# Moving a small-row store, recutting the last row and exchanging two waits at the end of a streaming row sum

## Chip, cores and metric

One core of one Trainium2 chip. Times are device microseconds (us) of that core, given as the median over runs. A run's time is about 1.35 us more than its *span*, from the first to the last instruction of the program; the profile shows the span. Trace times below count from the span's start; where three decimals stand, they are from the trace's records of instructions, packets and semaphore updates. In the views ACT is ScalarE, DVE is VectorE, and SPq and DVEq are the sequencers of SyncE and VectorE, which run waits and issue loads and stores; "issue" is time in which an engine waited for nothing that the profile shows. A *partial* is the sum of one piece of the last row; it is *announced* when its semaphore is updated, just after the short instruction that reads the accumulator out. A load or store has *landed* or is *complete* with the last of its 16 semaphore updates.

## The reference

```python
x = np.random.randn(32, 512, 1024).astype(np.float32)
def reference(x):
    return np.sum(np.maximum(x, 0), axis=-1).astype(np.float32)
```

16384 rows of 1024 numbers, 67.1 MB in and 64 KB out.

## The kernel before

Each of the 128 partitions takes 128 rows. They arrive in seven chunks of 16 rows, then in loads of 8, 4, 2 and 1 rows, and the very last row in three pieces of 512, 256 and 256 columns. All loads and stores are issued by SyncE on one queue. ScalarE sums the first piece of the last row; VectorE sums the second, then the third together with the two partial sums, which lie behind it in the same tile. Results leave in three stores: the middle rows (128 rows of 111 numbers, 444 bytes each), the first row of each partition (transposed, 4 rows of 128 bytes) and the last 16 rows (128 rows of 64 bytes).

```python
LAST = [512, 256, 256]
# ... loads of 8, 4, 2, 1 rows, then:
    parts = [buf[:, tb, r, 0:n0], buf[:, tb, r, n0:n1], last[:, 0 : LAST[2]]]
    for k, (lo, hi) in enumerate([(0, n0), (n0, n1), (n1, D)]):
        sp.dma_start(out=parts[k], in_=xv[-1][:, BIG - 1, lo:hi]).then_inc(
            s_in[NBIG + len(TAIL) + k], 16)
    sp.wait_ge(s_fact, 1)          # ScalarE is done with the big chunks
    sp.wait_ge(s_fdve, 1)          # VectorE too
    sp.dma_start(out=ov[1][:, :], in_=res[:, start[1] : start[2]]).then_inc(s_store, 16)
    sp.wait_ge(s_turn, 1)
    sp.dma_start(out=of[0:P].rearrange("(k q) -> k q", q=32),
                 in_=turned[0:P:32, 0:32]).then_inc(s_store, 16)
# ... all the work but the last row is cut ...
    n = LAST[2]
    act.wait_ge(s_in[-3], 16)
    on_act(parts[0], last[:, n : n + 1]).then_inc(s_part, 1)
    dve.wait_ge(s_in[-2], 16)
    on_dve(parts[1], last[:, n + 1 : n + 2]).then_inc(s_part, 1)
    dve.wait_ge(s_part, 2)
    dve.wait_ge(s_in[-1], 16)
    on_dve(last[:, :], res[:, J - 1 : J]).then_inc(s_tdve, 1)

    sp.wait_ge(s_tdve, 1)
    sp.dma_start(out=ov[-1][:, :], in_=res[:, start[-1] : J]).then_inc(s_out, 16)
    sp.wait_ge(s_store, 16 * (len(REGIONS) - 1))
    sp.wait_ge(s_out, 16)
```

In these programs' traces each computing or issuing instruction carries one wait at most. Of two waits in front of it, the one written *first* is built into the instruction, and the second becomes a wait instruction of its own ahead of it. So before the change VectorE waits separately for the last load, and its last instruction carries the wait for the two partials.

## Time and profile before

| | before |
|---|---|
| time, median of the first 3 runs (lowest to highest) | 161.03 us (160.97 to 161.25) |
| span of the profiled run | 159.908 us |

The prediction shows and reads the views of this profile: the chain of waits at the end, the timeline and the events of the last 2 us.

### The profile page before, as it was taken

The numbers are of one execution on the slowest core, as the hardware profiler recorded it, in microseconds if no ns is written. First come the engines' busy times: TensorE is split into PE (matmuls) and PEld (weight loads), VectorE is DVE, ScalarE is ACT, GpSimd is POOL, SyncE is SP. The second block draws the span as 40 slices with busy tenths as digits, with TensorE's granted clock in tenths as the row PEclk, the third lists the DMA queues.
The fourth block names the chain that finished last, engine by engine and source line by source line (L and its number), as shares of the span: only waits on it lengthen the run. The fifth ranks groups of instructions, "written<-read, shape, count | busy, mean of one in ns | idle before, by whom it ended". The sixth has DMA issues, their size and how long they took to land.

```text
span 159.9 us, 150 instructions
## 1 busy us (share of the span) xinstructions
DVE 121.5 (76%) x58; ACT 101.4 (63%) x55; POOL 0.2 (0%) x4
## 2 busy tenths in 40 slices
DVE  0000000999959999999969989699899999598995
ACT  3000059990799709996099942999339980496974
POOL 0000000000000000000000000000000000000000
DMA  9979996996996996997989969969969969899994
GB/s 377 492 338 400 492 525 262 525 525 262 525 525 262 525 525 262 525 459 328 525 361 426 525 262 525 525 262 525 525 262 525 525 262 525 369 418 393 408 381 148
DMA packets 2457, 67.18 MB, mean 420 GB/s; under 512 B 536, under 2 KB 792, under 8 KB 1176
## 3 DMA queue, kind: packets, MB, share of 16 engines
q1 hardware_dynamic: 2456, 67.18, 98.0%
q14 instruction: 1, 0.01, 0.0%
HBM read 67.11 MB, written 0.07 MB: 420 GB/s over the span
## 4 chain that ended last, share of the span: by engine, by line
DMA 68%; ACT 18%; DVE 11%; SPq 1%; issue 0%
DMA buf<-in_x_dram 68%; ACT buf L137 18%; DVE res L152 11%; SPq L98 1%; SPq L106 0%; DVE buf L122 0%; DVE last L122 0%
## 5 line engine op out<-in xcount | busy, mean ns | idle before, releaser
L152 DVE TENSOR_REDUCE res<-buf 128x7 f32<-128x7168 f32 (+4 forms) x16 | 100.0, 6281 | 33.7 <-ACT buf L137 33.7
L137 ACT ACTIVATE buf<-buf 128x7168 f32<-128x7168 f32 (+4 forms) x16 | 80.7, 5099 | 45.9 <-DMA buf<-in_x_dram 45.9
L119 ACT ACTIVATE buf<-buf 128x1024 f32<-128x1024 f32 (+1 forms) x19 | 19.0, 1000 | 9.3 <-DMA buf<-in_x_dram 9.3
L122 DVE TENSOR_SCALAR_CACHE_REDUCE buf<-buf 128x1024 f32<-128x1024 f32 (+2 forms) x19 | 20.9, 1147 | 3.1 <-DMA buf<-in_x_dram 2.9
L119 ACT ACTIVATION_READ_ACCUMULATOR buf<-buf 128x1 f32 x19 | 3.5, 186 | 0.0
L137 ACT ACT_TABLE_LOAD x1 | 1.3, 1283 | 1.3 <-PEq L216 1.3
L122 DVE DVE_READ_ACCUMULATOR buf<-buf 128x1 f32 x19 | 1.6, 84 | 0.0
L122 DVE TENSOR_SCALAR_CACHE_REDUCE last<-last 128x258 f32<-128x258 f32 x1 | 0.4, 422 | 0.0
L161 DVE STREAM_TRANSPOSE turned<-res 128x32 f32<-128x32 f32 x1 | 0.2, 211 | 0.0
L185 DVE TENSOR_TENSOR res<-half 128x1 f32<-128x1 f32 x1 | 0.2, 160 | 0.1
L216 POOL MEMSET const-bfloat16-1.0<- 128x1 bf16 x1 | 0.1, 102 | 0.0
L216 POOL MEMSET const-uint8-127<- 128x1 uint8 x1 | 0.1, 101 | 0.0
L216 POOL MEMSET const-float32-0.0<- 128x1 f32 x1 | 0.1, 99 | 0.2 <-issue 0.2
L216 POOL MEMSET const-float32-1.0<- 128x1 f32 x1 | 0.1, 98 | 0.0
L122 DVE DVE_READ_ACCUMULATOR last<-last 128x1 f32 x1 | 0.1, 83 | 0.0
## 6 DMA issues: line engine op xcount, KB each, us to landing
buf<-in_x_dram SPq DMA_DIRECT2D x1, 7680.0 KB, 21.2
buf<-in_x_dram SPq DMA_DIRECT2D x1, 4096.0 KB, 26.8
buf<-in_x_dram SPq DMA_DIRECT2D x1, 2048.0 KB, 31.3
buf<-in_x_dram SPq DMA_DIRECT2D x2, 512.0 KB, 18.9
buf<-in_x_dram SPq DMA_DIRECT2D x1, 1024.0 KB, 33.3
buf<-in_x_dram SPq DMA_DIRECT2D x1, 256.0 KB, 34.5
buf<-in_x_dram SPq DMA_DIRECT2D x1, 128.0 KB, 34.4
last<-in_x_dram SPq DMA_DIRECT2D x1, 128.0 KB, 34.2
```

The source lines that it names most:

```text
L98: sp.dma_start(out=buf[:, tb, r : r + n, :], in_=xv[-1][:, r : r + n, :]).then_inc(s_in[NBIG + i], 16)
L119: return act.activation(t, t, AF.Relu, accum_out=acc)
L122: return dve.tensor_scalar(out=t, in0=t, scalar1=0.0, scalar2=None, op0=ALU.max, op1=ALU.add, accum_out=acc)
L137: act.activation(t, t, AF.Relu).then_inc(s_act, 1)
L152: dve.tensor_reduce(out=res[:, c * BIG + r : c * BIG + r + n], in_=buf[:, c % NB, r : r + n, :], axis=X, op=ALU.add,).then_inc(s_dve, 1)
L161: dve.transpose(out=turned[:, :], in_=res[:, 0:32]).then_inc(s_turn, 1)
L185: dve.tensor_tensor(out=res[:, j0 + r : j0 + r + 1], in0=half[:, 0:1], in1=half[:, 1:2], op=ALU.add)
L216: nc = _bacc.Bacc("TRN2", target_bir_lowering=False, num_devices=1)
```

## The change

Its intent, as the diff shows it: keep the packets of 444 bytes out of the end of the load stream, have the second piece of the last row sooner, and let VectorE's last instruction answer the last load at once. Line numbers and blank lines apart, this is the whole diff:

```diff
-LAST = [512, 256, 256]
+LAST = [512, 224, 288]
@@ stores
-    sp.wait_ge(s_fact, 1)
-    sp.wait_ge(s_fdve, 1)
-    sp.dma_start(out=ov[1][:, :], in_=res[:, start[1] : start[2]]).then_inc(s_store, 16)
     sp.wait_ge(s_turn, 1)
     sp.dma_start(
         out=of[0:P].rearrange("(k q) -> k q", q=32), in_=turned[0:P:32, 0:32]
     ).then_inc(s_store, 16)
+    sp.wait_ge(s_fact, 1)
+    sp.wait_ge(s_fdve, 1)
+    sp.wait_ge(s_in[-2], 16)
+    sp.dma_start(out=ov[1][:, :], in_=res[:, start[1] : start[2]]).then_inc(s_store, 16)
@@ last row on VectorE
     on_dve(parts[1], last[:, n + 1 : n + 2]).then_inc(s_part, 1)
+    dve.wait_ge(s_in[-1], 16)
     dve.wait_ge(s_part, 2)
-    dve.wait_ge(s_in[-1], 16)
     on_dve(last[:, :], res[:, J - 1 : J]).then_inc(s_tdve, 1)
```

## The prediction

> **What bounds the kernel now.** I read the page's DMA rows first, then the chain of waits, then the timeline of the last 12 us, then the busy time by stretch around the last load. All times are in us from the span's start.
>
> The page's second and third parts (busy tenths of the DMA engines in 40 slices; the load queue's share of 16 engines) and the totals of its fourth part:
>
> ```profile
> DMA  9979996996996996997989969969969969899994
> ...
> q1 hardware_dynamic: 2456, 67.18, 98.0%
> ...
> DMA 68%; ACT 18%; DVE 11%; SPq 1%; issue 0%
> ```
>
> The DMA queue is busy for 98% of the span: the kernel streams 67.1 MB, and nothing in the diff changes those bytes. So the change can only act after the load stream runs dry. The end of the chain of waits (start, length, what) says what that tail is:
>
> ```profile
> 123.13 34.38 DMA buf<-in_x_dram
> 157.51 0.02 issue
> 157.53 0.44 DVE buf L122 x2
> 157.97 0.02 issue
> 158.00 0.43 DVE last L122 x2
> ```
>
> The last load but one lands at 123.13 + 34.38 = 157.51, VectorE sums its 256 columns, then the last 256 columns (plus the two partial sums, hence 258). The timeline of the tail (start, length, engine, line, operation) adds ScalarE and the stores:
>
> ```profile
> 147.26 0.35 SPq L111 DMA_DIRECT2D out_dram<-res  x1
> ...
> 157.17 0.63 ACT L119 ACTIVATE buf<-buf 128x512 f32<-128x512 f32 x1
> 157.27 0.16 DVE L185 TENSOR_TENSOR res<-half 128x1 f32<-128x1 f32 x1
> 157.53 0.42 DVE L122 TENSOR_SCALAR_CACHE_REDUCE buf<-buf 128x256 f32<-128x256 f32 x1
> 157.70 0.19 ACT L119 ACTIVATION_READ_ACCUMULATOR buf<-buf 128x1 f32 x1
> 157.88 0.08 DVE L122 DVE_READ_ACCUMULATOR buf<-buf 128x1 f32 x1
> 158.00 0.42 DVE L122 TENSOR_SCALAR_CACHE_REDUCE last<-last 128x258 f32<-128x258 f32 x1
> 158.34 0.08 DVE L122 DVE_READ_ACCUMULATOR last<-last 128x1 f32 x1
> 158.45 0.34 SPq L200 DMA_DIRECT2D out_dram<-res  x1
> ```
>
> From 158.45 to the end at 159.91 there is only the last store: 0.84 until its first packet at 159.29, 0.2 of packets, its last semaphore update at 159.864.
>
> The trace's semaphore records give three events that no line prints: the last load is complete at 157.859, ScalarE's partial is announced at 157.899, VectorE's own at 157.973. The last VectorE instruction starts at 157.997. So **it is not the last load that releases it but VectorE's own preceding sum**, 0.114 later. That 0.114 is all that reordering this tail can win, before any cost.
>
> Around the last load (columns: window, length, VectorE, ScalarE, Pool, clock, mean share of the DMA engines, GB/s):
>
> ```profile
> 156.50:157.00 0.50, 0.49 (x1) 0.49 (x1) 0.00 (x0) 1.00 1.06 371
> 157.00:157.20 0.20, 0.20 (x2) 0.20 (x3) 0.00 (x0) 1.00 1.09 376
> 157.20:157.40 0.20, 0.14 (x2) 0.20 (x2) 0.00 (x0) 1.00 1.02 298
> 157.40:157.60 0.20, 0.10 (x2) 0.20 (x1) 0.00 (x0) 1.00 0.35 87
> ```
>
> The rate drops after 157.2 while the engines stay busy. The packet records say why: the 128 packets of 444 bytes start between 157.117 and 157.606, although their store was issued at 147.26.
>
> **What the Trainium skill says.** (1) "DMA: Bandwidth & Descriptors", section "Queues, rings and completion order": on each DMA engine descriptors are consumed in ring order. The trace agrees: the store waited 9.9 us behind loads issued before it, and its packets begin where the first engines have finished theirs. (2) Same page, "Specifications": below 512 bytes a transfer loses line rate, through a read-modify-write. The trace agrees in direction only: a 444-byte packet took 25 ns (18 bytes per ns), a 1024-byte one 46 ns (22 bytes per ns); a read-modify-write itself is not to be seen. (3) "Perfetto Trace Analysis", "DVE / Act Engine Instruction": such an instruction is pushed into a hardware wait queue and waits there, so its decoding is over when the semaphore comes. A wait that the instruction does not carry is an instruction of its own in the sequencer, and the next one is decoded only after it. The trace agrees with the first half: from 157.510 (load complete) to 157.534 (VectorE starts) is 24 ns, and from 157.973 to 157.997 the same. For the second half it has separate waits on other engines: 47 to 68 ns from the end of one to the start of the next instruction (SyncE 147.209 to 147.256 and 1.205 to 1.273, ScalarE 1.210 to 1.265).
>
> **The change, part by part.** The built programs differ in order and waits only; VectorE and ScalarE have the same number of instructions. In the kernel before, VectorE's separate wait is for the last load and the last instruction carries the wait for the partial sums; afterwards it is the reverse.
>
> *Row split.* 32 columns move from the second piece to the third. A 256-column VectorE piece took 0.420 and a 512-column one 0.687, so a column costs (0.687 - 0.420) / 256 = 1.04 ns and 32 columns 0.033. In the stream, 256 columns took about 0.36 from landing to landing (157.144, 157.510, 157.859), so 32 columns are about 0.045: the second piece lands at about 157.465. VectorE is free (its addition ends at 157.429), starts at about 157.49, and announces its partial at 157.973 - 0.045 - 0.033 = 157.895. The total of bytes is the same, so the last load still lands at about 157.86. The last instruction has 290 columns instead of 258: +0.033, and this lies on the path.
>
> *Exchanged waits.* ScalarE's partial comes at 157.899, as before, and now ties with VectorE's. The separate wait begins some 25 ns later, at 157.92, and takes 0.02 (in the kernel before 157.886 to 157.907). Then the last instruction is decoded and finds the last load already there. With 0.047 to 0.068 for this step, an estimate from the other engines, it starts at 157.99 to 158.01, against 157.997 before. The 0.075 to 0.08 won by the smaller second piece is spent on the separate wait, because the load whose wait the instruction now carries is the *earlier* of the two events.
>
> *The store moved.* It leaves the place directly behind the loads. I follow the slowest DMA engine: its eight 1024-byte packets of the last load run at 42 to 47 ns each to the end (157.320, 157.363, 157.410), as those of the load ahead. So the stores of the other engines do not slow it visibly, and I credit at most 0.02. SyncE now waits for the second piece (157.465), issues the store at about 157.55 and is free at 157.9, well before it must issue the last store at 158.5. Its packets would run from about 157.55 + 0.84 = 158.39 to 158.6 or 158.7 on idle engines. With 0.4 to 0.5 from an engine's last packet to its semaphore update, as 12 of the 16 engines had in this trace, it is complete at about 159.1. The last store's packets come at about 159.33. No overlap, and the last event is still the last store. The 4-row store of the transposed sums, issued at about 124 instead of 147.65, stays behind the loads in the ring.
>
> *Sum.* Start of the last instruction +0.01, its length +0.033, the loads 0 to -0.02: about +0.02 to +0.04 on the end. The time before was 161.03, which makes 161.05.
>
> **Rivals.**
> (a) *The stores do slow the last load.* For it: the drop from 376 to 298 GB/s. Against: the slowest engine's packet rate, and semaphore updates that follow the packets by the same 0.40 as for the load ahead. If it is so, ScalarE's half row too would have to come earlier to help; 0.05 to 0.1 at most, a time of 160.95.
> (b) *The late store gets into the last store's way.* For it: the two are issued only about 0.95 apart, and four semaphore updates of the stores before came 1.0 after the 128-byte packets (158.469 to 158.508 against 157.384 to 157.473). If the late store needs that as well it ends at about 159.6, still ahead of 159.9; if writes queue, the last store ends 0.1 to 0.3 later: 161.2 to 161.3.
> (c) *A queue kept busy answers sooner.* The last store's 0.84 from issue to first packet comes after 1.7 us of idle DMA engines; the late store shortens that idle time to about 0.7. The skill ("DMA: Bandwidth & Descriptors", "Latency and other measured facts") gives about 600 ns to the first byte on this path. Were 0.84 to become that, 0.2 would be gained: 160.8. Nothing in this trace shows that idleness costs anything.
> (d) *The exchanged wait is cheap on VectorE.* If the separate wait costs nothing after 157.92, the instruction starts near 157.95: 161.00.
>
> **Range and chances.** Every rival moves the end by 0.3 at most, which is 0.2% of 161; 2% would be 3.2 us, more than the whole tail after the last load (159.91 - 157.86 = 2.05). The three runs before spread over 0.28. I take 160.75 to 161.35. Faster or slower by over 2% has about half a per cent each.
>
> **What would show it.** In the changed kernel: the last load lands within 0.02 of 157.86 after the same start of the stream (rival a if earlier); the 290-column instruction takes about 0.455 and starts 0.08 to 0.12 after the later partial sum (rival d if about 0.05); the 444-byte packets run near 158.4 to 158.7 and are complete before 159.3 (rival b if the last store's time from issue to landing grows above 1.41, rival c if it shrinks below 1.3). I am wrong if the span moves by more than 0.3, above all if the stream itself ends at another time because of the 896- and 1152-byte rows.

## The result, and the profile after

161.11 us (160.98 to 161.65, 6 runs) against 161.02 us (160.94 to 161.25, 6 runs) for the kernel before; ratio 1.0008, 95% interval 0.9993 to 1.0023. A ratio is the mean time of one kernel's fast runs over that of the other's in the same rounds, so it is not quite the ratio of the medians. The interval holds 1, so the timing shows no difference; that the change costs anything rests on the traces below.

The end of the chain of waits of the changed kernel (start, length, what), which answers to the five lines that the prediction shows of before:

```profile
122.24 34.03 DMA buf<-in_x_dram
156.28 0.02 issue
156.30 1.41 ACT buf L120 x4
157.71 0.03 issue
157.74 0.02 DVEq L196
157.76 0.07 issue
157.83 0.46 DVE last L123 x2
```

Two things are new. The chain now runs through ScalarE instead of VectorE. And between the last partial (157.71) and the last instruction (157.83) there is a step of VectorE's sequencer, the separate wait of line 196, with 0.03 ahead of it and 0.07 after it. Before, 0.02 stood between the two.

The timeline of the same stretch:

```profile
157.28 0.39 DVE L123 TENSOR_SCALAR_CACHE_REDUCE buf<-buf 128x224 f32<-128x224 f32 x1
157.35 0.34 SPq L116 DMA_DIRECT2D out_dram<-res  x1
157.51 0.19 ACT L120 ACTIVATION_READ_ACCUMULATOR buf<-buf 128x1 f32 x1
157.60 0.08 DVE L123 DVE_READ_ACCUMULATOR buf<-buf 128x1 f32 x1
157.83 0.46 DVE L123 TENSOR_SCALAR_CACHE_REDUCE last<-last 128x290 f32<-128x290 f32 x1
...
158.32 0.34 SPq L201 DMA_DIRECT2D out_dram<-res  x1
```

The two partials are ready together (157.70 and 157.68), as intended; the last load was complete at 157.581. So the load whose wait the last instruction now carries had been there for 0.25 when the instruction began. From the last load to the end it is 2.192 us, against 2.049 before.

A trap lies in these two profiles: the span of the changed kernel is *shorter*, 159.773 against 159.908, though its median time is longer. Its last load landed 0.278 earlier. 0.22 of that lies between the landing of the two-row load (155.000 and 154.994) and of the one-row load (156.275 and 156.489), ahead of anything the change touches. So single spans can't be compared at this scale. What can be compared is the stretch after a fixed event, and for the timing many runs.

### The profile page after: what moved, and what is told of

It reads as the page before. It is cut to its first block, busy times and chain, and to the rows that moved or that the text cites. A ratio compares the mean times of both kernels' runs of the same rounds, so it can differ in the third digit from the quotient of the medians.

```text
span 159.8 us, 150 instructions
## 1 busy us (share of the span) xinstructions
DVE 121.5 (76%) x58; ACT 101.5 (64%) x55; POOL 0.2 (0%) x4
## 4 chain that ended last, share of the span: by engine, by line
DMA 68%; ACT 18%; DVE 11%; SPq 1%; issue 0%; DVEq 0%
DMA buf<-in_x_dram 68%; ACT buf L138 18%; DVE res L153 11%; ACT buf L120 1%; SPq L98 1%; DVE last L123 0%; DVEq L196 0%
## 5 line engine op out<-in xcount | busy, mean ns | idle before, releaser
L123 DVE TENSOR_SCALAR_CACHE_REDUCE last<-last 128x290 f32<-128x290 f32 x1 | 0.5, 456 | 0.1
```

What stands on the lines that cost most here:

```text
L123: return dve.tensor_scalar(out=t, in0=t, scalar1=0.0, scalar2=None, op0=ALU.max, op1=ALU.add, accum_out=acc)
```

## The experiments

Twelve runs were made, two of them repeats without an edit; all gave the right result. A, B and C come from one profiled execution of each. The tails are compared by three intervals. **A**: from the landing of the 512-column piece, with which ScalarE's path begins, to the end of the span. **B**: from the end of the later partial sum's accumulator read to the start of VectorE's last instruction. **C**: from the last load's landing to the end of the span. Times are medians with the number of runs; "of before" is the kernel before in the same rounds.

| kernel | A | B | C | time (n) | of before | ratio, 95% interval |
|---|---|---|---|---|---|---|
| before (first profile) | 2.764 | 0.035 | 2.049 | | | |
| before_again | 2.754 | 0.034 | 2.077 | 160.94 (5) | 161.03 | 0.9996, 0.9982 to 1.0009 |
| store_only | 2.744 | 0.034 | 2.088 | 160.97 (5) | 161.03 | 0.9997, 0.9985 to 1.0010 |
| waits_only | 2.853 | 0.131 | 2.188 | 161.07 (5) | 161.03 | 1.0006, 0.9993 to 1.0018 |
| split_store | 2.714 | 0.032 | 2.075 | 160.98 (5) | 161.03 | 0.9999, 0.9986 to 1.0011 |
| split_only | 2.868 | (load last) | 2.067 | 160.94 (5) | 160.99 | 0.9996, 0.9982 to 1.0010 |
| the change | 2.820 | 0.128 | 2.192 | 161.11 (6) | 161.02 | 1.0008, 0.9993 to 1.0023 |
| after_again | 2.809 | 0.130 | 2.150 | 161.14 (5) | 161.08 | 0.9998, 0.9986 to 1.0010 |
| store_later | 2.807 | 0.128 | 2.172 | 161.05 (5) | 160.99 | 1.0005, 0.9993 to 1.0018 |
| one_sem | 2.713 | 0.032 | 2.088 | 161.28 (5) | 160.99 | 1.0017, 1.0004 to 1.0030 |
| one_sem_no_spare | 2.731 | 0.033 | 2.094 | 161.27 (6) | 161.08 | 1.0016, 1.0004 to 1.0029 |
| one_sem_padded | 2.713 | 0.033 | 2.054 | 160.89 (5) | 161.08 | 0.9989, 0.9977 to 1.0001 |
| one_sem_448 | | 0.035 | 2.073 | 161.46 (5) | 160.99 | 1.0028, 1.0016 to 1.0041 |
| wide_last | | 0.130 | 2.185 | 161.01 (5) | 161.08 | 0.9992, 0.9979 to 1.0005 |

The timing alone can't separate these kernels: every interval holds 1, but for three single-wait kernels whose excess lies outside the span (below). The intervals A, B and C can, because they repeat: A of the kernel before is 2.764 and 2.754, of the changed kernel 2.820 and 2.809; B is 0.035 and 0.034 against 0.128 and 0.130. As repeats differ by 0.01 in A, a difference of 0.01 to 0.02 there is not shown to be one.

**before_again**: no edit.

> The kernel before once more, for its profile. The two profiles at hand differ in a place that the change should not touch: from the landing of the two-row load (154.994 before, 155.000 after) to that of the last load took 2.865 us before and 2.581 after. Theory (chance in the stream): this stretch differs by 0.1 to 0.3 us from the first profile of the same kernel, up or down. Rival (the stores queued behind the loads slow it): it is 2.8 to 2.9 us again. Time ratio 1.000 under both.

2.788 us: 0.08 less than the first time, a little under the theory's 0.1 to 0.3, and just under the rival's 2.8, so it decides nothing. The slow place is the stretch from the two-row to the one-row load, 1.495 and 1.411 in the two profiles of the kernel before and 1.27 to 1.28 in waits_only and split_only, which have the stores in the same place. So stores in that place don't make it slow by themselves, and chance fits. Shown it is not: both slow profiles are among the four with the stores directly behind the loads, and the ten profiles with the store moved all have 1.26 to 1.28.

**store_only** (diff abridged):

```diff
+    sp.wait_ge(s_turn, 1); <store of the transposed row>     # first
     sp.wait_ge(s_fact, 1); sp.wait_ge(s_fdve, 1)
+    sp.wait_ge(s_in[-2], 16)
     <store of 444-byte rows>
```

> Only the store is moved, row split and VectorE's waits as before. Theory: worth nothing on the path; the last VectorE instruction starts about 0.02 to 0.03 us after VectorE's own partial sum as before, the late store is complete (its last semaphore update) at least 0.5 us before the last store's; time ratio 0.999 to 1.001. Rival a (the stores slow the last loads): the stretch from the two-row load to the last load is 2.6 us or less, and the time 0.2 us shorter, ratio 0.9985. Rival b (the late store gets in the last store's way): the last store takes over 1.45 us from issue to landing instead of 1.41, ratio over 1.001.

A is 0.01 to 0.02 shorter, B unchanged, the ratio inside the theory's range. The last store took 1.398 us, so rival b falls. The late store was complete 0.27 us before the last one, not 0.5: it took 1.979 us from issue. The stretch from the two-row load was 2.633, but 2.636 in waits_only with the stores in their old place, so it says nothing for rival a. The packet records speak against it directly: from the end of the 512-column piece's last packet to the end of the last load's last packet it takes 0.689, 0.689, 0.689 and 0.693 us in the four kernels with the store behind the loads, and 0.717, 0.693, 0.693 and 0.696 in store_only, split_store, the change and after_again. So the store's packets don't delay the last packet of the loads. The announcements agree less: from the landing of the 512-column piece to that of the last load it takes 0.665 to 0.801 us in those four kernels, and 0.625 to 0.659 in the eight with the store moved and a 512-column piece. Since the last load is not what the end waits for in the kernel before, this could cost the path little; by A the whole move is worth 0.02 at most.

**waits_only**:

```diff
-    dve.wait_ge(s_part, 2)
     dve.wait_ge(s_in[-1], 16)
+    dve.wait_ge(s_part, 2)
     on_dve(last[:, :], res[:, J - 1 : J]).then_inc(s_tdve, 1)
```

> Only VectorE's two waits are exchanged, row split and stores as before. VectorE's own partial, announced about 0.11 us after the last load, is then met by a separate wait. Theory: the last instruction starts 0.10 to 0.14 us after that partial instead of 0.024, so the end is 0.09 us later, ratio 1.0005. Rival (the separate wait is cheap, the order of waits does not matter): 0.02 to 0.04 us as before, ratio 1.000.

The end of its chain of waits, and then that of before_again:

```profile
157.16 0.44 DVE buf L122 x2
157.60 0.03 issue
157.63 0.02 DVEq L195
157.65 0.07 issue
157.72 0.43 DVE last L122 x2
```

```profile
157.25 0.44 DVE buf L122 x2
157.68 0.02 issue
157.71 0.43 DVE last L122 x2
```

The same two pieces of work, the same 0.43 at the end, and 0.12 between them instead of 0.02 (B counts from 0.01 earlier, the end of the accumulator read). A grew by 0.09 to 0.10. The theory holds, and this part alone costs more in A than the whole change does (0.055).

**split_store**: the changed kernel, with the waits in their old order:

```diff
-    dve.wait_ge(s_in[-1], 16)
     dve.wait_ge(s_part, 2)
+    dve.wait_ge(s_in[-1], 16)
```

> The changed kernel with VectorE's two waits in their old order: row split and store moved. Theory: the last instruction starts 0.02 to 0.05 us after the later of the two partials, or 0.1 after the last load where that is later, so 0.05 to 0.1 us sooner than in the changed kernel against the same event; with 0.033 us for 32 more columns it ends 0.02 to 0.06 us sooner than the kernel before does against its last load. Ratio 0.9995 to 1.000. Rival (the order of waits does not matter): 0.12 us after the later partial as in the changed kernel, ratio 1.0005.

B is 0.032 and A 2.714, 0.04 to 0.05 under the kernel before and 0.10 under the changed kernel, as the theory had it against the same event. Against the last load (C) it ends 2.075 after, not sooner than the kernel before: the two ranges of the expectation are about different events, and this one missed. The end of its chain of waits:

```profile
156.25 1.41 ACT buf L120 x4
157.66 0.02 issue
157.68 0.46 DVE last L123 x2
```

The step of the sequencer is gone. Split and moved store help a little, and the exchanged waits more than take it back.

**split_only**: `LAST = [512, 224, 288]` alone.

> Only the row split is changed to 512, 224, 288; stores and VectorE's waits as before. Theory: ScalarE's partial now comes last of the two, about 0.75 us after its own piece landed; the last VectorE instruction starts 0.02 to 0.03 after the later partial and 0.12 to 0.15 after the last load, takes 0.455, and the end of the span is 2.06 to 2.10 us after the last load, as in the kernel before (2.05 and 2.08). With the stores directly behind the loads the stretch from the landing of the 512-column piece to that of the last load tells whether they cost anything: 0.63 to 0.64 us as with the store moved away means nothing, 0.66 to 0.70 means 0.02 to 0.06. Time ratio 0.999 to 1.001.

This run fell out of the pattern in a useful way. One DMA engine announced its part of the last load 0.205 us after the fifteenth had, so the load came 0.046 after the later partial, and A (2.868) is longer for that. From the 512-column piece to the last load it took 0.801, more than either range of the expectation; why that engine was late stays open, the stores behind the load included. The instruction started 0.174 after the later partial, not 0.02 to 0.03. The chain shows it:

```profile
123.52 34.05 DMA last<-in_x_dram
157.57 0.03 issue
157.60 0.02 DVEq L195
157.62 0.07 issue
157.69 0.46 DVE last L122 x2
```

With the waits in their old order the separate wait is the one for the load; here the load came last (157.570), and the same 0.12 lies between it and the instruction. So the cost belongs to the separate wait, not to one of the events.

**store_later** (diff abridged): the changed kernel, with

```diff
-    sp.wait_ge(s_in[-2], 16)
+    sp.wait_ge(s_part, 2)
     <store of 444-byte rows>
```

> The changed kernel, but the store of 444-byte rows waits for the two partial sums instead of the last load but one, about 0.42 us later. In three runs it took 1.81 to 1.98 us from issue to its last semaphore update, the last store 1.41. Theory (the two stores do not disturb each other; what counts is which ends last): the late store is issued about 0.1 us after the last partial and ends 1.8 to 2.0 later, which is level with the last store's end or up to 0.15 us after it; the last store still takes 1.39 to 1.43; the stretch from the last load to the end grows from 2.19 to 2.2 to 2.35 us, time ratio 1.0005 to 1.002. Rival (writes that follow each other closely queue): the last store itself takes 1.5 us or more.

The stores, in its timeline:

```profile
157.62 0.34 SPq L116 DMA_DIRECT2D out_dram<-res  x1
...
158.14 0.33 SPq L201 DMA_DIRECT2D out_dram<-res  x1
```

Issued 0.52 us apart, the last store still took 1.399 us: the rival falls. But the theory's size missed too. The late store was not level with the last one, it was complete 0.315 before it, 1.603 us after its issue, and C is 2.172 instead of 2.2 to 2.35. Over all profiles with the moved store that time ranges from 1.60 to 2.09; what decides it stays open. It never set the end.

**one_sem**: the changed kernel, with one wait for all three events:

```diff
-    on_act(parts[0], last[:, n : n + 1]).then_inc(s_part, 1)
+    on_act(parts[0], last[:, n : n + 1]).then_inc(s_in[-1], 1)
-    on_dve(parts[1], last[:, n + 1 : n + 2]).then_inc(s_part, 1)
+    on_dve(parts[1], last[:, n + 1 : n + 2]).then_inc(s_in[-1], 1)
-    dve.wait_ge(s_in[-1], 16)
-    dve.wait_ge(s_part, 2)
+    dve.wait_ge(s_in[-1], 18)
```

> The changed kernel with one wait in place of two: the partial sums add 1 each to the semaphore of the last load, and VectorE's last instruction carries the wait for 18. Theory (the separate wait costs 0.1 us, whichever event it is for): the last instruction starts 0.02 to 0.04 us after the last of the three events instead of 0.12, so the stretch from the last load to the end is 2.07 to 2.12 us instead of 2.19; time ratio about 0.9995 of before. Rival (VectorE needs 0.1 us after its own accumulator read anyway): the start stays 0.1 us or more after the last partial, 2.19 us.

The end of its chain of waits:

```profile
156.08 1.42 ACT buf L120 x4
157.50 0.02 issue
157.52 0.46 DVE last L123 x2
```

The step of the sequencer is gone, B is 0.032 and C 2.088: the theory holds in the trace. The time does not follow (ratio 1.0017, 0.9995 was expected): four of the five runs took 161.23 to 161.47 us with spans of 159.6 and 159.7, so 1.63 to 1.87 us lay outside the span instead of 1.3 to 1.4. Only the profiled run had 1.40.

**one_sem_448**: the same with `LAST = [448, 248, 328]`.

> The same single wait with the row cut into 448, 248 and 328 columns, so that both partial sums come at or before the last load (ScalarE's 0.14 us sooner against it). Theory: the last instruction starts 0.02 to 0.05 us after the last load and takes 0.422 + 70 x 1.04 ns = 0.495 us; from the last load to the end 2.00 to 2.04 us, the shortest of all kernels, 0.15 us under the changed kernel and 0.05 under the kernel before; time ratio about 0.9995, too little for the timing to tell. Rival (partials still last): the stretch is 2.07 or more.

C is 2.073, so here the rival's size came out: VectorE's partial still ended 0.065 after the last load, and the instruction started 0.100 after it instead of 0.02 to 0.05. The time outside the span was 1.54 to 1.88 us again.

**after_again**: no edit. **one_sem_no_spare**: one_sem without the allocation of `s_part`. **one_sem_padded**: one_sem with one more wait on VectorE, long satisfied, ahead of the seventh chunk of 16 rows (it ran at 137.7, 22 us before the end, not 10):

```diff
     for c in range(NTWO, NBIG):
         act.wait_ge(s_in[c], 16 * len(CHUNKS[c]))
+        dve.wait_ge(s_in[0], 16 * len(CHUNKS[0]))
         dve.wait_ge(s_in[c], 16 * len(CHUNKS[c]))
```

> The changed kernel once more, beside the next three. Theory (the exchanged wait costs 0.1 us and nothing else in the change is worth anything): from the last partial to the start of the last VectorE instruction 0.11 to 0.13 us, from the last load to the end of the span 2.17 to 2.22 us (2.05 to 2.08 in the kernel before), time ratio 1.0000 to 1.0012. Rival (the 0.09 us of the first comparison was chance): 2.05 to 2.10, ratio 0.9995 or less.

B is 0.130 again; C is 2.150, a little under the range. The ratio, 0.9998, is below the theory's range although its interval covers it. The trace repeats, the timing is too coarse.

> The single wait again (512, 224, 288), without the semaphore that had fallen out of use. The first time its tail was 2.09 us as expected, but its timed runs took 0.3 to 0.5 us more outside the span (time less span 1.4 to 1.9 us instead of 1.3 to 1.4). Theory (the unused semaphore is not the reason): tail 2.07 to 2.12 again, and time less span again 1.4 to 1.9, ratio 1.001 to 1.003. Rival (the unused semaphore was, or it was chance): time less span 1.3 to 1.4, ratio 0.9990 to 0.9998.

> The single wait, with one more separate wait put on VectorE 10 us before the end, on a load that landed long ago, so that VectorE has as many instructions as in the kernel before. Theory (the extra time outside the span comes from the program being one instruction shorter): time less span 1.3 to 1.4 us again, tail 2.07 to 2.12, so ratio 0.9990 to 0.9998. Rival (it comes from the shared semaphore): 1.4 to 1.9, ratio 1.001 to 1.003.

Without the unused semaphore the excess stays (1.65 to 1.96 us outside the span); with one more instruction it is gone (1.33 to 1.39). The tail of the padded kernel, 2.054, and its ratio, 0.9989, are each just under the ranges expected. The pages of the two show what moved, first one_sem_no_spare (its first line and packets), then one_sem_padded (with its instruction queue, which the other page lacks):

```profile
span 159.7 us, 149 instructions
...
DMA packets 2456, 67.18 MB, mean 421 GB/s; under 512 B 536, under 2 KB 792, under 8 KB 1176
```

```profile
span 159.5 us, 150 instructions
...
DMA packets 2457, 67.18 MB, mean 421 GB/s; under 512 B 536, under 2 KB 792, under 8 KB 1176
...
q14 instruction: 1, 0.01, 0.0%
```

With 150 instructions one packet of 8 KB from the instruction queue falls inside the span (at 159.306, 0.15 before the end). With 149 none does; after the start, the trace has such packets only at 161.23 and 161.38, 1.5 us and more after the end (in one_sem one at 160.79, 1.3 after; that execution was the one with 1.40). The semaphore records agree: in the three profiles with 149 instructions the zeroing of semaphores 153 to 203, after the program's end, begins 0.60 us after the span and is over at 1.12, in the eleven others it begins at 0.30 to 0.33 and is over at 0.64. That something waits for its next instructions outside the span fits all this, and the padding shows that the program's length, not the shared semaphore, brings it. The engine that waits is not named in the records.

**wide_last**: the changed kernel with `LAST = [416, 240, 368]`.

> The changed kernel with the row cut into 416, 240 and 368 columns, so that the partials come before the last load and the order of the change's waits fits: the separate wait for the partials is over when the last load lands. Theory: the last instruction starts 0.02 to 0.08 us after the last load and takes 0.422 + 110 x 1.04 ns = 0.536 us; the tail is 2.04 to 2.10 us, 0.1 under the changed kernel and level with the kernel before; ratio 0.999 to 1.000. Rival (exchanging the waits costs 0.1 us whatever the order of events): start 0.1 us or more after the last load, tail over 2.13.

C is 2.185 and the start 0.160 after the last load: the theory's numbers missed. But the run doesn't decide: the second piece landed only 0.405 before the last load, so VectorE's partial ended 0.03 after it, where I had wanted it before. Measured from that partial, B is again 0.130. The order of events that would suit the exchanged waits was never reached.

**Best version.** one_sem_padded has the shortest span of all profiles (159.460, as one_sem) and the lowest median, 160.89 us; its interval still holds 1, so it isn't shown to beat the kernel before. Its tail is 0.10 shorter than the changed kernel's by interval A, and that is shown.

## Why the prediction was right or wrong

*The bound, right.* The stream sets all but the last 2 us; no variant moved the time by more than 0.3%. 161.05 was predicted, 161.11 and 161.14 were measured, inside the range. That is no test of the other terms: the range of 160.75 to 161.35 also holds the medians of the kernel before and of eleven of the twelve runs.

*The row split, right.* The 290-column instruction took 0.456 (0.455 predicted), and the two partials tied within 0.02 (157.692 and 157.709). Split together with the moved store is worth -0.04 to -0.05 in A.

*The exchanged waits: mechanism right, size a little short.* The separate wait began 0.027 after the later partial and took 0.021, as estimated from before; from its end to the instruction it was 0.071, where I had taken 0.047 to 0.068 from other engines. By itself the exchange costs 0.09 to 0.11 (waits_only against the two profiles of before; the change against split_store, 2.820 - 2.714).

*The sum, right in sign by the traces, too small.* I had +0.02 to +0.04, which the timing can't tell from nothing. In A the change costs 2.820 - 2.764 = 0.056, and 0.055 for the repeated pair. It is made up of -0.02 (store, 2.764 to 2.744, 0.01 against the repeat, so hardly more than the spread), -0.03 (split, 2.744 to 2.714) and +0.11 (waits).

*"The last load still lands at about 157.86", wrong as put.* It landed at 157.581, and at 157.542 in the same kernel before, run again. By the prediction's own sign an earlier landing spoke for rival (a). The sign was a bad one: from the landing of the two-row load to that of the last it took 2.865 before and 2.581 after, but 2.636 in waits_only, with the stores in their old place. The place of one landing varies by 0.3 from one execution to the next, and the first profile had a slow one. That also made it look as if ScalarE's partial came only 0.04 after the last load; in the repeat it was 0.08, in the changed kernel 0.13 and 0.09 to 0.10. So the event whose wait became separate was late by more than I had assumed, and C grew by 0.07 to 0.14, where my sum would have given 0.02 to 0.04. What decides the place of the last landing, the stores behind it included, stays open.

*The moved store, right.* First packet 0.844 after issue (0.84), complete at 159.159 and in the repeat 159.237 (159.1), last store 1.410 and 1.400.

*The packets below 512 bytes: no step to be seen.* The prediction took 18 bytes per ns at 444 bytes against 22 at 1024 as agreeing in direction with the page's mark at 512 bytes. But the usual packet times of the kernels before and after, 11, 13, 25, 41, 46, 51, 84 and 2418 ns for 64, 128, 444, 896, 1024, 1152, 2048 and 65536 bytes, lie within 3 ns of one line, 8.65 ns and 0.0368 ns more per byte (an estimate from these). Small packets are slow here for the fixed part alone.

*Rivals.* (a) fell as to the packets and the path (0.02 at most); the announcements leave it open for the landing of the last load. (b) fell: the last store took 1.40 to 1.42 in all kernels with the late store. (c) fell: 0.831 from the last store's issue to its first packet, 0.836 before, though the engines' idle time ahead of it was 0.63 instead of 1.66. (d) fell: 0.12 from the later partial's announcement to the start (0.13 from the end of its read) instead of 0.05.

## What to carry to other kernels

Where an instruction has two waits and, as in these programs, only one rides on it, give that place to the event that comes *last by the trace* (0.03 us from it to the instruction, against 0.13), or put the events on one semaphore with one sum to wait for, which took 0.10 us out of this tail; here that made the program one instruction shorter, which cost more outside the span until a wait was added. Check which event is last in more than one profile: here two runs of the same kernel put the last load 0.3 us apart, and a recut of the row changes the order again. When a change leaves the trace shorter and the time longer, compare the time outside the span before doubting the trace.

## What the Trainium skill lacked or had wrong

- No page has the price of a second wait on VectorE. From the end of the partial's accumulator read to the start of the waiting instruction: 0.032 to 0.035 us when the instruction carries the wait, 0.128 to 0.131 when the wait is separate; the same 0.12 after a load (split_only).
- "Runtime: NRT & Kernel Launch", section "Instruction fetch mechanics", calls the cost of crossing a block of instructions mostly hidden. Here a program of one instruction fewer had its last recorded 8 KB fetches after the end of the span instead of 0.15 us before it, and 1.5 to 2.0 us outside the span in 15 of 16 runs instead of 1.3 to 1.4; one more instruction brought it back. Whether such a crossing is what costs here, no record shows.
- "DMA: Bandwidth & Descriptors", section "Latency and other measured facts", has about 600 ns to the first byte on this path. From the start of a store's issuing instruction to its first packet, with nothing queued ahead, these runs show 0.82 to 0.86 us, and for the last store 0.825 to 0.843 whether the engines had been idle for 0.18 us (store_later) or 1.9 us (split_only). Counted from the end of that instruction it is 0.49 to 0.51 us; the section doesn't say which start it means.
